# A logarithm series, a table load, two convolution inputs and two weight splits moved in the first layer of a Trainium2 encoder kernel

## The chip, the cores and the metric

One Trainium2 chip, one of its cores. The metric is the device time of one execution in microseconds (us). The kernel before takes 1221.76 us, the median of 3 runs (1221.18 to 1223.83).

The engines are named as the profile names them: PE is the matrix engine (PEld its weight loads), DVE the vector engine, ACT the scalar engine with its function tables, POOL the general engine, SP the queue that issues loads. Each works through its own instructions in order and waits for the others by semaphores. PSUM is the memory that PE writes to, here 8 banks of 128 x 512 float32; everything else lies in SBUF. "Wh" and "wl" below are the two halves into which a float32 weight is split so that PE can multiply it.

## The reference

Two layers on 512 positions of width 1024. Layer 0 mixes with a gated linear recurrence (RG-LRU), layer 1 with stick-breaking attention; each is followed by a SwiGLU block of width 2816, with an RMS norm ahead of every block and at the end. Only layer 0's mixer is touched by the change:

```python
h = rmsnorm(x, g)                       # rsqrt of the mean square, per position
gate_br, x_br = split(h @ w_in)         # 1024 + 1024 columns
xc = causal_conv(x_br, conv_w) + conv_b # 4 taps along the positions
r = sigmoid(blockdiag(xc, w_r) + b_r)   # 4 blocks of 256
i = sigmoid(blockdiag(xc, w_i) + b_i)
log_a = 8 * r * log_sigmoid(lam)        # lam: one number per channel
a = exp(log_a)
u = sqrt(max(-expm1(2 * log_a), 0)) * (i * xc)
hs = scan(a, u)                         # h_t = a_t h_{t-1} + u_t
x = x + (hs * gelu(gate_br)) @ w_out
```

## The kernel before, in words

Everything is kept transposed: 128 channels on the partitions, 512 positions along the row. A 128 x 1024 piece of weights is a *chunk*. SP loads it (raw), ACT copies it to a rounded half (wh, L136), and DVE or POOL subtracts that from the raw data (wl, L137). A product is then three matmuls for each 128 x 128 block: wh by the high half of the input (L165), wh by the low half (L166), wl by the high half (L167). Three buffers each for wh and wl and four for raw limit how far this runs ahead. Which engine makes wl is written down for the first 20 chunks in a table, `wl_on` (L58), and alternates afterwards.

Layer 0's mixer is the function `rglru`, and its chunks come in this order: m = 0 to 6 of the x branch (chunks 0 to 6), the gate weights of block 0 (7), m = 7 (8), gate weights of block 1 (9), then g = 0 and 1 of the gate branch (10, 11), gate weights of block 2 (12), g = 2 (13), gate weights of block 3 (14), g = 3 to 7 (15 to 19), and then the 8 chunks of the output product. PE takes them in that order, without a break if its inputs are there and its target bank is free. Banks are handed out in turn: x tiles 0 to 3 go to banks 70 to 73, the norm's sums to 74, x tile 4 to 75, the broadcast to 76, tiles 5 and 6 to 77 and 70; the gates of block 0 take 71 to 74, tile 7 takes 75 again, the gates of block 1 76, 77, 70, 71, g = 0 and 1 take 72 and 73, the gates of block 2 74 to 77, g = 2 takes 70, the gates of block 3 71 to 74. A bank can be written again only when its last reader is done.

The norm is not applied to the input. ACT squares the input tiles (L235), DVE adds the squares up (`acc`, L237), and in the middle of tile 3 PE sums `acc` over the partitions (`norm_rs1`, L255). ACT takes the square root of the sum (L242), DVE refines its reciprocal in five small operations (L243 to L247) and writes it on four diagonals (L249). In the middle of tile 4 PE multiplies the diagonals with ones (`norm_rs2`, L263), ACT copies the result (L264): `rsB`, the factor of each position, the same in all partitions. Every x tile is multiplied with it when it is taken out of PSUM.

That is `evac_x` (L324): DVE multiplies bank and rsB (L330), into a tile `xb` in SBUF for m < 4 and in place in PSUM for the others; ACT writes the first tap and the bias to xc (L331); DVE adds the three other taps to xc, one operation each (L333); ACT rounds xc (ah, L335), DVE subtracts (al, L336). For m < 4 the bank is free after the first of these, for the others after the third tap.

`decay` (L310) computes 8 log_sigmoid(lam) for 8 columns of 128 channels: a reciprocal, a square, and a series of ten terms in Horner's form, a multiplication and an addition for each term, all on 128 x 8 elements, each step on the result of the one before. Its result is first needed by the gates of block 0.

After the gates (sigmoids on ACT, L357 and L358, and a multiplication on POOL, L359), `chain` computes a and the square root on ACT and the scans on DVE (L373, L374), four tiles at a time. The gate branch's tiles are multiplied by rsB on DVE (`gt`, L432) and, for g < 5, kept in SBUF so that the bank is free.

The scheduler orders each engine's instructions by the program's order, priorities and `tc.issue_after`, which holds instructions back until a given one has been placed.

Of the kernel before, what the change touches and what calls it, by code (L numbers as in the profile page):

```python
# [13 lines left out]
AF = mybir.ActivationFunctionType  # L14
ALU = mybir.AluOpType
# [23 lines left out]
def ts(i, n=P):  # L39
    return slice(i * n, (i + 1) * n)  # L40


class Kern:
    def __init__(self, ctx, tc, a, out):
        self.ctx, self.tc, self.nc, self.a, self.out = ctx, tc, tc.nc, a, out
        mk = lambda name, bufs, **kw: ctx.enter_context(tc.tile_pool(name=name, bufs=bufs, **kw))
        self.const = mk("const", 1)
        self.wp = mk("wp", 1)
        self.tp = mk("tp", 1)
        self.ar = mk("ar", 1)  # L50
        self.free = deque(range(NSLOT))
        self.slot = {}
        pp = mk("pp", 1, space=bass.MemoryType.PSUM)
        self.bank = [pp.tile([P, S], F32, name=f"bank{i}") for i in range(8)]
        self.bi = 0
        self.tn = 0
        self.wl_dve = False
        self.wl_on = {**dict.fromkeys((*range(5, 12), 14, 15, 16), self.nc.gpsimd),  # L58
                      **dict.fromkeys((2, 3, 4, 12, 13, 17, 18, 19), self.nc.vector)}

    def ps(self):
        b = self.bank[self.bi % 8]
# [235 lines left out]
    def rglru(self):  # L298
        nc, tc = self.nc, self.tc
        with ExitStack() as cx:  # L300
# [4 lines left out]
            cl, w, z, z2, pl = (sm[:, ts(i, 8)] for i in range(5))  # L305
# [4 lines left out]
            def decay():  # L310
                nc.vector.tensor_scalar(z, w, 2.0, None, ALU.add)
                nc.vector.reciprocal(z, z)
                nc.vector.tensor_tensor(z, z, w, ALU.mult)
                nc.vector.tensor_tensor(z2, z, z, ALU.mult)
                nc.vector.tensor_scalar(pl, z2, 2.0 / 21, 2.0 / 19, ALU.mult, ALU.add)
                for n in (17, 15, 13, 11, 9, 7, 5, 3, 1):
                    nc.vector.tensor_tensor(pl, pl, z2, ALU.mult)
                    nc.vector.tensor_scalar(pl, pl, 2.0 / n, None, ALU.add)
                nc.vector.tensor_tensor(pl, pl, z, ALU.mult)
                nc.vector.scalar_tensor_tensor(cl, lam, 0.0, pl, ALU.min, ALU.subtract)  # L320
                nc.vector.tensor_scalar(cl, cl, RG_C, None, ALU.mult)
                nc.vector.tensor_scalar(ncl, cl, -1.0, 0.0, ALU.mult, ALU.max)

            def evac_x(m, ps):  # L324
                xc[m], ah[m], al[m] = self.new("xc"), self.new("ah", F32R), self.new("al", F32R)
                cw = lambda j: self.col("cw", j * 8 + m)
                src = ps
                if m < 4:
                    ps = self.new("xb")
                nc.vector.tensor_tensor(ps, src, self.rsB, ALU.mult)  # L330
                nc.scalar.activation(xc[m], ps, AF.Identity, scale=cw(3), bias=self.col("cb", m))  # L331
                for d in (1, 2, 3):
                    nc.vector.scalar_tensor_tensor(xc[m][:, d:], ps[:, :S - d], cw(3 - d), xc[m][:, d:],  # L333
                                                   ALU.mult, ALU.add)
                nc.scalar.copy(ah[m], xc[m])  # L335
                nc.vector.tensor_tensor(al[m], xc[m], ah[m].bitcast(F32), ALU.subtract)  # L336
                if m < 4:
                    self.rel(ps)

            def tile_x(m, mid=None):  # L340
                p = self.ps()
                self.mm_tile(p, self.u, mid)
                return p

            def gates(n, prev=None):
                wh, wl = self.chunk()
                for j in range(2):
                    m = 2 * n + j
                    pr, pi = self.ps(), self.ps()
                    for g, pt in ((0, pr), (1, pi)):  # L350
                        for k in range(2):
                            o = (g * 2 + j) * 2 + k
                            self.mm3(pt, wh[:, ts(o)], wl[:, ts(o)], ah[2 * n + k], al[2 * n + k], k == 0, k == 1)
                    r[m], sv[m] = self.new("r"), self.new("sv")
                    iv = self.tmp()
                    with tc.issue_after(prev.ins) if prev else ExitStack():
                        nc.scalar.activation(r[m], pr, AF.Sigmoid, bias=self.col("br", m))  # L357
                        nc.scalar.activation(iv, pi, AF.Sigmoid, bias=self.col("bi", m))  # L358
                    nc.gpsimd.tensor_tensor(xc[m], iv, xc[m], ALU.mult)  # L359
                    self.last = nc.scalar.activation(sv[m], r[m], AF.Tanh, scale=ncl[:, m:m + 1])  # L360
# [28 lines left out]
            def tile_x2():  # L389
                p = (self.ps(), self.ps())  # L390
                raws = [self.raw.pop(i)[0] for i in range(2)]
                hl = [self.split_tiles(i) for i in range(2)]
                for k in range(KT):
                    self.norm_in(k, "g_mix0", False)
                    for i in range(2):
                        if k % 2 == 0:
                            self.split_piece(i, raws[i], *hl[i], slice(k * P, (k + 2) * P))
                        self.mm3(p[i], hl[i][0][:, ts(k)], hl[i][1][:, ts(k)], *self.u[k], k == 0, k == KT - 1)
                for i in range(2):
                    self.wq.pop(i)  # L400
                self.used = 2
                return p

            pend = []
            for m in range(KT):
                if m == 0:
                    with tc.manual_schedule(engines={mybir.EngineType.Activation, mybir.EngineType.DVE}):
                        pend = list(enumerate(tile_x2()))
                    continue
                if m == 1:  # L410
                    continue
                pend.append((m, tile_x(m, {3: self.norm_rs1, 4: self.norm_rs2}.get(m))))
                if m == 2:
                    with tc.issue_after(self.uhi.ins):
                        for k in range(KT):
                            self.norm_sq(k, nc.vector)
                elif m == 3:
                    with tc.issue_after(self.dgi.ins):
                        decay()
                if m >= 4:  # L420
                    for q in pend[:3]:
                        evac_x(*q)
                    pend = pend[3:]
                if m in (6, 7):
                    gates(m - 6)
            for q in pend:
                evac_x(*q)
# [430 lines left out]
```

## Time and profile before

| what | us |
|---|---|
| median of 3 runs | 1221.76 |
| the profiled execution, as a run | 1221.93 |
| its span, first to last instruction | 1220.1 |
| PE busy in it | 1167.0 |
| DVE, ACT and POOL busy in it | 586.0, 521.4, 463.8 |

Between the run's time and the span lie 1.8 us. The times of instructions below count from the start of the span. A row of the timeline gives start, duration, engine, line, operation, output and inputs, and in square brackets the idle time of the engine before it and who ended it; "x3" is three like operations in a row, merged. A matmul's duration overlaps with the next one's, so what counts for PE is the distance from start to start.

### The profile page before, as it was taken

The page shows a single profiled execution, that of the slowest core. Times are in us where ns is not written, and L with a number is a line of the kernel's source. Part 1 is how long each engine was busy: PE and PEld are TensorE (multiplying, and loading weights), DVE is VectorE, ACT ScalarE, POOL GpSimd, SP SyncE. Part 2 cuts the span into 40 slices and gives each one's busy share as a digit, 9 for nine tenths or more (in the row PEclk, how much of TensorE's full clock was granted, in tenths as well). Part 3 has the DMA queues.
Part 4 walks back from the last instruction along what each step waited for, and adds up shares of the span by engine and source line. Part 5 has one row for each costly group of instructions (what it writes and reads, how often), then busy time and mean ns, then how long its engine had stood idle before and what let it go on. Part 6 is the DMA issues. An engine that isn't in the chain of part 4 may idle for free.

```text
span 1220.1 us, 13748 instructions
## 1 busy us (share of the span) xinstructions
PE 1167.0 (96%) x5347; PEld 956.8 (78%) x5347; DVE 586.0 (48%) x797; ACT 521.4 (43%) x750; POOL 463.8 (38%) x285
## 2 busy tenths in 40 slices
PE   9899999999999999999978888799999999999996
PEld 6687788888888888888866766578888888888886
DVE  6977743323323222222799999985332332321112
ACT  6497443323323222223677777654332332332221
POOL 2353343333333323321166666524333333332332
PEclk9999999999999999999999999999999999999998
DMA  7222322232322333332111011113223232233321
GB/s 243 70 84 84 100 97 93 97 99 91 104 96 93 93 97 95 98 103 91 52 48 36 35 35 53 35 53 103 94 96 100 90 104 96 93 93 97 95 63 69
DMA packets 31313, 105.80 MB, mean 87 GB/s; under 512 B 3600, under 2 KB 4624, under 8 KB 31248
## 3 DMA queue, kind: packets, MB, share of 16 engines
q1 hardware_dynamic: 30960, 104.40, 26.6%
q8 instruction: 42, 0.69, 0.2%
q10 hardware_dynamic: 288, 0.52, 0.1%
q14 instruction: 23, 0.19, 0.0%
HBM read 102.81 MB, written 2.10 MB: 86 GB/s over the span
## 4 chain that ended last, share of the span: by engine, by line
PE 74%; DVE 13%; issue 3%; ACT 2%; POOL 0%; DVEq 0%; ACTq 0%; POOLq 0%
PE bank L165 24%; PE bank L167 24%; PE bank L166 24%; DVE sph L637 2%; DVE t L636 2%; DVE wl L137 2%; DVE r L643 1%; DVE awh L679 1%; PE bank L663 1%; DVE ql L591 1%; DVE ks L598 1%; DVE t L577 1%; DVE o L702 1%; DVE awl L684 1%; DVE bank L382 0%
## 5 line engine op out<-in xcount | busy, mean ns | idle before, releaser
L136 ACT CAST wh<-raw 128x1024 fp32r<-128x1024 f32 (+2 forms) x202 | 203.3, 1009 | 534.5 <-PE bank L166 281.0
L165 PE MATMUL bank<-uh,wh 128*128 128x512 f32 x960 | 377.8, 394 | 13.7 <-DVE t L577 8.1
L167 PE MATMUL bank<-uh,wl 128*128 128x512 f32 x960 | 374.5, 390 | 1.0 <-DVE wl L137 1.0
L166 PE MATMUL bank<-ul,wh 128*128 128x512 f32 x960 | 374.7, 390 | 0.3 <-DVE ul L220 0.3
L137 POOL TENSOR_TENSOR wl<-raw,wh 128x1024 fp32r<-128x1024 f32 (+2 forms) x97 | 225.6, 2326 | 366.8 <-ACT wh L136 362.5
L165 PEld LDWEIGHTS bank<-uh,wh 128*128 128x128 f32 x960 | 181.0, 188 | 53.3 <-issue 15.2
L167 PEld LDWEIGHTS bank<-uh,wl 128*128 128x128 f32 x960 | 180.6, 188 | 39.3 <-DVE wl L137 1.4
L166 PEld LDWEIGHTS bank<-ul,wh 128*128 128x128 f32 x960 | 180.9, 188 | 37.8 <-DVE ul L220 0.9
L137 DVE TENSOR_TENSOR wl<-raw,wh 128x1024 fp32r<-128x1024 f32 (+2 forms) x105 | 132.6, 1266 | 139.4 <-ACT wh L136 138.4
L469 POOL TENSOR_TENSOR fl<-t,fh 128x512 fp32r<-128x512 f32 x44 | 67.3, 1529 | 198.1 <-ACT fh L468 198.1
L165 PE MATMUL bank<-fh,wh 128*128 128x512 f32 (+1 forms) x374 | 141.1, 377 | 0.0
L166 PE MATMUL bank<-fl,wh 128*128 128x512 f32 (+1 forms) x374 | 140.8, 376 | 0.0
L167 PE MATMUL bank<-fh,wl 128*128 128x512 f32 (+1 forms) x374 | 140.8, 376 | 0.0
L465 DVE TENSOR_TENSOR t<-bank,rsB 128x512 f32<-128x512 f32 x44 | 30.4, 691 | 199.4 <-PE bank L167 199.4
L463 DVE TENSOR_TENSOR t<-bank,rsB 128x512 f32<-128x512 f32 x44 | 30.4, 691 | 117.1 <-PE bank L167 117.1
L638 POOL TENSOR_TENSOR spl<-t,sph 128x512 fp32r<-128x512 f32 (+1 forms) x48 | 58.9, 1231 | 65.4 <-DVE sph L637 51.6
L165 PEld LDWEIGHTS bank<-fh,wh 128*128 128x128 f32 x374 | 70.4, 188 | 13.0
L166 PEld LDWEIGHTS bank<-fl,wh 128*128 128x128 f32 x374 | 70.4, 188 | 12.8
L167 PEld LDWEIGHTS bank<-fh,wl 128*128 128x128 f32 x374 | 70.4, 188 | 12.8
L237 POOL TENSOR_TENSOR acc<-acc,t 128x512 f32<-128x512 f32 x24 | 38.6, 1608 | 52.1 <-ACT t L235 43.4
L684 POOL TENSOR_TENSOR awl<-t,awh 128x512 fp32r<-128x512 f32 x28 | 40.0, 1427 | 41.2 <-DVE awh L679 41.2
L491 DVE TENSOR_TENSOR x<-x,bank 128x512 f32<-128x512 f32 x15 | 10.3, 687 | 74.7 <-PE bank L167 74.7
(165 smaller groups left out, 1464.3 us busy)
## 6 DMA issues: line engine op xcount, KB each, us to landing
raw<-w_gu SPq DMA_DIRECT2D x88, 512.0 KB, 3.5
raw<-w_dn SPq DMA_DIRECT2D x32, 448.0 KB, 3.3
raw<-w_dn SPq DMA_DIRECT2D x16, 512.0 KB, 3.5
raw<-w_qk SPq DMA_DIRECT2D x16, 512.0 KB, 3.4
raw<-w_in SPq DMA_DIRECT2D x14, 512.0 KB, 3.7
raw<-w_ao SPq DMA_DIRECT2D x8, 512.0 KB, 3.5
raw<-w_v SPq DMA_DIRECT2D x8, 512.0 KB, 3.4
raw<-w_bo SPq DMA_DIRECT2D x8, 512.0 KB, 3.4
```

Source lines behind the costliest of these rows:

```text
L136: self.nc.scalar.copy(wh[:, c], raw[:, c])
L137: self.wl_engine(i).tensor_tensor(wl[:, c], raw[:, c], wh[:, c].bitcast(F32), ALU.subtract)
L165: mm(out, lhsT=wh, rhs=xh, start=first, stop=False)
L166: mm(out, lhsT=wh, rhs=xl, start=False, stop=False)
L167: mm(out, lhsT=wl, rhs=xh, start=False, stop=last)
L237: self.acci = eng.tensor_tensor(self.acc, self.acc, sq, ALU.add)
L463: nc.vector.tensor_tensor(tg, pg, self.rsB, ALU.mult)
L465: nc.vector.tensor_tensor(tu, pu, self.rsB, ALU.mult)
L469: nc.gpsimd.tensor_tensor(al[f], tu, ah[f].bitcast(F32), ALU.subtract)
L636: nc.vector.scalar_tensor_tensor(sp[:, :w], z, 0.0, e[:, :w], ALU.max, ALU.add)
L638: nc.gpsimd.tensor_tensor(sl[:, :w], sp[:, :w], sh[:, :w].bitcast(F32), ALU.subtract)
L684: eng.tensor_tensor(wl[:, :w], ts_[i][:, :w], hd["wh"][i][:, :w].bitcast(F32), ALU.subtract)
```

## The change

Four edits.

- The series: each term is now one operation, (pl + 2/n) * z2, where it was a multiplication and an addition: 27 small operations become 18.
- The series is issued behind the last addition of `acc` (`acci`), no longer behind the last diagonal (`dgi`).
- ACT takes the root of one dummy element behind the squares, so that the table of the square root is loaded there and not in front of L242.
- The tiles m = 2 and 3 are multiplied by rsB in place in PSUM, as m = 4 to 7 were; `xb` is left for m = 0 and 1. The wl of chunks 15 and 16 (g = 3 and 4) goes from POOL to DVE.

```diff
-        self.wl_on = {**dict.fromkeys((*range(5, 12), 14, 15, 16), self.nc.gpsimd),
-                      **dict.fromkeys((2, 3, 4, 12, 13, 17, 18, 19), self.nc.vector)}
+        self.wl_on = {**dict.fromkeys((*range(5, 12), 14), self.nc.gpsimd),
+                      **dict.fromkeys((2, 3, 4, 12, 13, 15, 16, 17, 18, 19), self.nc.vector)}
...
-                nc.vector.tensor_scalar(pl, z2, 2.0 / 21, 2.0 / 19, ALU.mult, ALU.add)
-                for n in (17, 15, 13, 11, 9, 7, 5, 3, 1):
-                    nc.vector.tensor_tensor(pl, pl, z2, ALU.mult)
-                    nc.vector.tensor_scalar(pl, pl, 2.0 / n, None, ALU.add)
-                nc.vector.tensor_tensor(pl, pl, z, ALU.mult)
+                nc.vector.tensor_scalar(pl, z2, 2.0 / 21, None, ALU.mult)
+                for n in (19, 17, 15, 13, 11, 9, 7, 5, 3):
+                    nc.vector.scalar_tensor_tensor(pl, pl, 2.0 / n, z2, ALU.add, ALU.mult)
+                nc.vector.scalar_tensor_tensor(pl, pl, 2.0, z, ALU.add, ALU.mult)
...
-                if m < 4:
+                if m < 2:
                     ps = self.new("xb")
...
-                if m < 4:
+                if m < 2:
                     self.rel(ps)
...
                         for k in range(KT):
                             self.norm_sq(k, nc.vector)
-                elif m == 3:
-                    with tc.issue_after(self.dgi.ins):
+                        nc.scalar.activation(self.st[:, 0:1], self.ones[:, 0:1], AF.Sqrt)
+                    with tc.issue_after(self.acci.ins):
                         decay()
```

From here on lines of the changed kernel are one lower than before from L318 on: L329 there is L330 here, L332 is L333, L335 is L336, L431 is L432.

Where the series stands on DVE before, between the norm's sums and the first x tile (sm holds the series' values, st and rsT the norm's):

```order
L237 TENSOR_TENSOR acc<-acc,t_300 128x512
L243 TENSOR_SCALAR st<-bank_74 128x4
L244 RECIPROCAL st<-st 128x4
L245 SCALAR_TENSOR_TENSOR st<-st 128x4
L246 TENSOR_TENSOR st<-st 128x4
L247 SCALAR_TENSOR_TENSOR rsT<-st 128x4
L249 TENSOR_SCALAR t_325<-ident,rsT 128x128 x4
L311 TENSOR_SCALAR sm<-sm 128x8
L312 RECIPROCAL sm<-sm 128x8
```

The same place on DVE in the changed kernel, four small steps (L312 to L315) left out at the dots:

```order
L237 TENSOR_TENSOR acc<-acc,t_300 128x512
L311 TENSOR_SCALAR sm<-sm 128x8
...
L317 SCALAR_TENSOR_TENSOR sm<-sm 128x8 x7
L243 TENSOR_SCALAR st<-bank_74 128x4
L317 SCALAR_TENSOR_TENSOR sm<-sm 128x8
L244 RECIPROCAL st<-st 128x4
...
L247 SCALAR_TENSOR_TENSOR rsT<-st 128x4
L320 TENSOR_SCALAR sm<-sm 128x8
L249 TENSOR_SCALAR t_344<-ident,rsT 128x128
L321 TENSOR_SCALAR sm<-sm 128x8
L249 TENSOR_SCALAR t_344<-ident,rsT 128x128 x3
```

Twelve steps of the series now stand ahead of the norm's first small operation, and the other six between its operations; none stands behind the last diagonal.

The x tiles 2 to 4 on DVE in the changed kernel, from the third tile's second tap on (xc_42, xc_45 and xc_48 are tiles 2, 3 and 4; the bank's number is the last two digits):

```order
L332 SCALAR_TENSOR_TENSOR xc_42_424<-bank2_72,par_86,xc_42_424 128x510
L329 TENSOR_TENSOR bank3_73<-bank3_73,rsB_129 128x512
L332 SCALAR_TENSOR_TENSOR xc_42_424<-bank2_72,par_86,xc_42_424 128x509
L329 TENSOR_TENSOR bank5_75<-bank5_75,rsB_129 128x512
L332 SCALAR_TENSOR_TENSOR xc_45_464<-bank3_73,par_86,xc_45_464 128x511
L335 TENSOR_TENSOR al_44_426<-xc_42_424,ah_43_425 128x512
L332 SCALAR_TENSOR_TENSOR xc_45_464<-bank3_73,par_86,xc_45_464 128x510
L332 SCALAR_TENSOR_TENSOR xc_48_474<-bank5_75,par_86,xc_48_474 128x511
L332 SCALAR_TENSOR_TENSOR xc_45_464<-bank3_73,par_86,xc_45_464 128x509
L332 SCALAR_TENSOR_TENSOR xc_48_474<-bank5_75,par_86,xc_48_474 128x510
```

The order of the tiles is that of before; what moved is what they read: before, the rows of tiles 2 and 3 read xb, and bank 73 was free after its first row.

The scans of tiles 2 and 3 and what follows them on DVE, before:

```order
L374 SCALAR_TENSOR_TENSOR sv_72_666<-r_71_665,xc_46_473 128x512
L432 TENSOR_TENSOR gt_79_762<-bank3_73,rsB_129 128x512
L432 TENSOR_TENSOR gt_86_838<-bank0_70,rsB_129 128x512
L137 TENSOR_TENSOR wl17_945<-raw17_812,wh17_944 128x1024
L368 SCALAR_TENSOR_TENSOR sv_81_783<-t93_885,sv_81_783 128x512
```

and in the changed kernel:

```order
L373 SCALAR_TENSOR_TENSOR sv_70_656<-r_69_655,xc_45_464 128x512
L431 TENSOR_TENSOR gt_77_752<-bank3_73,rsB_129 128x512
L137 TENSOR_TENSOR wl15_831<-raw15_726,wh15_830 128x1024
L431 TENSOR_TENSOR gt_84_828<-bank0_70,rsB_129 128x512
L137 TENSOR_TENSOR wl16_903<-raw16_758,wh16_902 128x1024
L137 TENSOR_TENSOR wl17_935<-raw17_802,wh17_934 128x1024
```

The two wl stand behind the multiplication of g = 1, the one that frees bank 73, and are gone from POOL, where they stood ahead of the multiplications by the input gate of tiles 5 and 6.

## The prediction

> **What bounds the kernel now.** I read the page first, then the waits of PE over the first 160 us, which hold the mixer, then the timelines of PE, DVE, POOL and ACT around each wait.
>
> ```profile
> PE 1167.0 (96%) x5347; PEld 956.8 (78%) x5347; DVE 586.0 (48%) x797; ACT 521.4 (43%) x750; POOL 463.8 (38%) x285
> ...
> PE bank L165 <- DVE xc L333: 5.4, 1, 5.4
> PE bank L165 <- DVE gt L432: 1.5, 1, 1.5
> ...
> PE bank L166 <- DVE al L384: 1.1, 1, 1.1
> PE bank L167 <- DVE wl L137: 1.0, 1, 1.0
> ```
>
> PE is busy in 96% of the span, and behind the mixer nothing is edited: what PE loses by waiting in the mixer is lost at the end, and what it no longer loses is gained. In the mixer it waits four times for more than 1 us or about that: for a third tap of the convolution, for the multiplication of g = 1, and later for al and wl. The rows of PE at the first two:
>
> ```profile
> 32.89 1.06 PE L263 MATMUL bank<-t,ones 128*128 128x128 f32 x8
> ...
> 50.15 0.39 PE L165 MATMUL bank<-ah,wh 128*128 128x512 f32 x1
> ...
> 52.65 0.39 PE L167 MATMUL bank<-ah,wl 128*128 128x512 f32 x1
> 58.39 0.77 PE L165 MATMUL bank<-uh,wh 128*128 128x512 f32 x1 [5.36 <-DVE xc L333]
> ...
> 62.07 0.40 PE L165 MATMUL bank<-uh,wh 128*128 128x512 f32 x1
> ...
> 95.20 0.39 PE L167 MATMUL bank<-ah,wl 128*128 128x512 f32 x1
> 97.13 0.50 PE L165 MATMUL bank<-ah,wh 128*128 128x512 f32 x1 [1.54 <-DVE gt L432]
> ```
>
> From 50.15 to 52.65 there are 11 steps, 0.227 us each. The matmul at 62.07 is the tenth of tile 7; without a break it would have started at 52.65 + 10 x 0.227 = 54.92. So the first wait costs 7.15 us: 5.51 of waiting and 1.64 because PE comes back slow (nine steps in 3.68 us, 0.41 each). The second wait costs 97.13 - 95.43 = 1.70 and 0.11 more for a first matmul of 0.50 in place of 0.39: 1.81 us, with no slow stretch behind it.
>
> Why the third tap of tile 4 is late is in DVE's rows, beside those of POOL:
>
> ```profile
> 21.70 3.08 DVE L237 TENSOR_TENSOR acc<-acc,t 128x512 f32<-128x512 f32 x4
> 27.79 0.16 DVE L243 TENSOR_SCALAR st<-bank 128x4 f32<-128x4 f32 x1 [3.01 <-ACT st L242]
> 27.87 0.17 DVE L244 RECIPROCAL st<-st 128x4 f32<-128x4 f32 x1
> ...
> 31.11 0.17 DVE L318 TENSOR_SCALAR sm<-sm 128x8 f32<-128x8 f32 x1
> 31.32 2.36 DVE L317 TENSOR_TENSOR sm<-sm 128x8 f32<-128x8 f32 x1
> ...
> 36.04 0.68 DVE L330 TENSOR_TENSOR xb<-bank,rsB 128x512 f32<-128x512 f32 x1
> ...
> 39.45 2.38 DVE L322 TENSOR_SCALAR sm<-sm 128x8 f32<-128x8 f32 x1
> ...
> 50.33 0.69 DVE L330 TENSOR_TENSOR bank<-bank,rsB 128x512 f32<-128x512 f32 x1
> 50.93 0.74 DVE L333 SCALAR_TENSOR_TENSOR xc<-xb,par,xc 128x511 f32<-128x511 f32 x1
> 51.59 0.68 DVE L336 TENSOR_TENSOR al<-xc,ah 128x512 fp32r<-128x512 f32 x1
> 52.19 0.74 DVE L333 SCALAR_TENSOR_TENSOR xc<-xb,par,xc 128x510 f32<-128x510 f32 x1
> 52.85 0.74 DVE L333 SCALAR_TENSOR_TENSOR xc<-bank,par,xc 128x511 f32<-128x511 f32 x1
> 53.51 2.22 DVE L333 SCALAR_TENSOR_TENSOR xc<-xb,par,xc 128x509 f32<-128x509 f32 x1
> ...
> 57.51 0.74 DVE L333 SCALAR_TENSOR_TENSOR xc<-bank,par,xc 128x509 f32<-128x509 f32 x1
> ```
>
> ```profile
> 24.88 2.38 POOL L137 TENSOR_TENSOR wl<-raw,wh 128x1024 fp32r<-128x1024 f32 x1 [10.77 <-ACT wh L136]
> 31.27 2.39 POOL L137 TENSOR_TENSOR wl<-raw,wh 128x1024 fp32r<-128x1024 f32 x1 [4.01 <-ACT wh L136]
> ...
> 52.85 2.34 POOL L137 TENSOR_TENSOR wl<-raw,wh 128x1024 fp32r<-128x1024 f32 x1 [4.24 <-PE bank L166]
> ...
> 90.40 2.85 POOL L137 TENSOR_TENSOR wl<-raw,wh 128x1024 fp32r<-128x1024 f32 x1
> 93.21 2.21 POOL L359 TENSOR_TENSOR xc<-t,xc 128x512 f32<-128x512 f32 x1
> ```
>
> Three things are seen. DVE has no gap here from 36.04 on and starts its tiles only when the series lets it. A DVE operation that takes all its data from SBUF stands still while POOL works: 0.17 us become 2.36 beside POOL's 31.27, a *hold* of 2.2 us; the tap from xb at 53.51 takes 2.22 instead of 0.74. And the tap from a bank at 52.85, under the same POOL operation, takes 0.74: with a PSUM input there is no hold.
>
> **The change part by part.** Steps from start to start: L330 50.33 to 50.93, 0.60; a tap 0.66 (50.93 to 51.59); al 0.60 (51.59 to 52.19); a small step that needs the one before 0.205 (31.11 to 31.32), one that doesn't 0.08 (27.79 to 27.87).
>
> *The table.* ACT's rows, with the broadcast's copy and the first bias of tile 7, used below:
>
> ```profile
> 23.75 1.05 ACT L136 CAST wh<-raw 128x1024 fp32r<-128x1024 f32 x1 [1.85 <-PE bank L166]
> 24.82 1.28 ACT L242 ACT_TABLE_LOAD   x1
> ...
> 33.98 0.59 ACT L264 COPY rsB<-bank 128x512 f32<-128x512 f32 x1 [2.79 <-PE bank L263]
> ...
> 67.88 0.78 ACT L331 ACTIVATE xc<-bank,par 128x512 f32<-128x512 f32 x1 [1.30 <-DVE bank L330]
> ```
>
> Before, the load ran from 24.82 to 26.10 and the root waited on for PE's sums: hidden. Now 1.28 and a dummy of a few tenths lie in the 1.85 us in which ACT waits for PE anyway. Worth nothing either way; were the gap missing, the wh behind it would come up to 1.5 us later, for a chunk that PE needs only with tile 5, whose turn comes after 32.89, the middle of tile 4.
>
> *The series.* It starts at 24.7 behind the last addition, in DVE's gap of 3.01. Its second operation, at 24.9, meets POOL's 24.88 and is held to about 27.28. Ten dependent steps later, at 27.3 + 9 x 0.205 = 29.2, comes L243 (before: 27.79). The norm's and the series' operations now alternate and hide each other's delay, 0.205 a pair: five pairs bring the first diagonal to 30.25, the three others at 0.22 each end near 31.1. PE wants them at 32.89, so this costs nothing, with 1.8 us to spare, but only 0.15 us before POOL's 31.27. Behind the diagonals nothing is left of the series; rsB is there at 34.57, and the first L330 starts at 34.6 instead of 36.04. L322's hold at 39.45 is not saved: POOL's next wl then stops a tap from xb.
>
> *Two more tiles in PSUM.* Their six taps can no longer be held; the price is that banks 72 and 73 are free only after the third tap. By the order of the changed kernel, up to tile 3's third tap DVE does 5 multiplications, 13 taps and 3 al: 5 x 0.60 + 13 x 0.66 + 3 x 0.60 = 13.38, and one hold of 2.2 among the taps from xb: 15.6. From 34.6 that gives 50.18 for the next start, and the tap itself ends 0.08 later, 50.26. PE wants bank 73 for the gates of block 0 at 50.15: a wait of 0.15 with the semaphore, and 0.11 for the restart. Bank 72 is needed at 48.8 and free at 46.4. Tile 4's third tap follows after 2 x 0.66 + 2 x 0.60 = 2.52, ending at 52.8, where before it began at 57.51; PE wants bank 75 at 52.88, now 53.1. The wait of 5.36 is gone, and with it the slow stretch: 7.15 - 0.26 = 6.9 us gained.
>
> [...]
>
> *The two wl.* The second wait is for g = 1's multiplication, behind two multiplications and two scans that POOL holds:
>
> ```profile
> 83.03 2.33 DVE L374 TENSOR_TENSOR_SCAN sv<-r,xc 128x512 f32<-128x512 f32 x2
> ...
> 86.39 4.59 DVE L373 TENSOR_TENSOR xc<-xc,sv 128x512 f32<-128x512 f32 x2
> 90.91 5.59 DVE L374 TENSOR_TENSOR_SCAN sv<-r,xc 128x512 f32<-128x512 f32 x2
> 96.42 1.25 DVE L432 TENSOR_TENSOR gt<-bank,rsB 128x512 f32<-128x512 f32 x2
> ```
>
> Two scans without POOL take 2.33. Without the wl of 90.40 POOL goes straight to the multiplication now at 93.21 (1.2 us by itself), from 91.0 to 92.2, and the scans end at 94.4: g = 1's multiplication starts at 94.4 instead of 96.42 and ends at 95.1, against PE's wish at 95.43. These are times of before; ACT, DVE and POOL all move forward with tile 7, PE with its own gain. PE gains 6.9; the chain starts with ACT's bias of tile 7, at 67.88 before. I carry the queue on from 52.8: taps and al of tiles 4 to 6 to 58.15, two al that alternate with two POOL multiplications to 60.6, L329 to 61.3: 6.6 earlier. So 0.3 of PE's lead is not matched, the slack of 0.3 covers it, and I leave 0.15 for a restart: 1.81 - 0.15 = 1.65 gained. The wl themselves add 2 x 1.2 us to DVE behind that point, before the wl of chunk 17, for which DVE waits idle already; PE needs chunk 15 only after block 3's gates. The waits for wl and al later in the mixer hang on chains that start with PE's block 3 gates: they move with PE and stay.
>
> Sum: 6.9 + 1.65 = 8.5 us. The profiled execution, 1221.93, stands 0.17 above the median; from the median, 1221.76 - 8.5 = **1213.2**.
>
> **The rivals.** *The diagonals miss the gap* (0.14). If the series takes 0.2 us longer than I add up, POOL's 31.27 catches one to four diagonals until 33.5; PE then waits at 32.89, 0.9 to 1.6 us, and rsB and everything behind it shift with PE, so that it is paid once: up to 1214.8. The 0.15 us of margin speak for it. [...]
>
> *The second wait stays* (0.11). If the chain of tile 7 gains less than PE, g = 1 is late as before: 1221.76 - 6.9 = 1214.9.
>
> *The wait moves to bank 73* (0.10). If DVE is held twice more before tile 3's third tap, that is 4.4 us, PE waits 4.5 for bank 73, and, as that is near the wait after which it was slow, loses another 1.6: 1219.3, which is no gain that can be told; with one hold, about 1215.5. The sum above has no reserve: 50.26 against 50.15.
>
> *Slower* (0.03). The series ahead of the diagonals makes the broadcast the bound: from a delay of about 11 us at 32.89 on, more than the 8.5 gained and 2.4. That would need about 1.1 us for each of the 12 small steps ahead of L243; they take 0.205, and two holds together make 4.4.
>
> *More* (0.04). The wait for wl at about 118, 1.0 and a restart, goes too: 8.96 + 1.1 gives 1211.7.
>
> **How the numbers follow.** The forecast, 1212.5 to 1214.2 as the two remainders are 0 or 1 us, has 0.58. The range takes in the better case, the first two rivals and the milder half of the third: 1211.6 to 1216.8. A measurement of this kernel tells about 0.2%, 2.4 us, from no change: faster needs less than 1219.3. The third rival at its worst and a failure of the series' move give 0.05 for the same, 0.03 for slower, 0.92 for faster.
>
> **What would show it.** In the new profile: no wait of PE for a tap above 0.5 us, no steps of 0.41 behind it; the first L329 at 34.6; the diagonals done before 31.27; tile 3's third tap ending near 50.3; no row of `gt` among PE's waits. A PE wait at L263, or DVE rows of 2.2 us and more among the taps from a bank, would prove me wrong.

## The result and the profile after

| | before | after |
|---|---|---|
| median, us (4 runs each) | 1221.47 | 1214.55 |
| lowest to highest | 1220.34 to 1223.83 | 1211.87 to 1214.85 |
| the profiled execution, its span | 1221.93, 1220.1 | 1214.85, 1213.1 |
| mixer stretch in it | 108.25 | 100.56 |

The changed kernel is faster by 0.6%: ratio of the runs 0.9936, 95% interval 0.9916 to 0.9956 (the two medians alone give 0.9943). Forecast were 1213.2 us, 0.9930 of the 1221.76 known then, and a range of 1211.6 to 1216.8. "Mixer stretch" is used for all kernels below: from PE's first matmul behind the norm's sums (L255) to the last matmul of the mixer that PE had to wait for (before: from 27.32 to 135.57). From there to the first matmul of the SwiGLU block it is 38.7 us in both. The stretch is the better measure of a small edit, since the start of L255 itself lies anywhere from 25.88 to 29.19 us in the profiles of this study, and at 27.32 and 27.92 in two profiles of one and the same kernel. It goes in part with the landing of the second of x's eight tiles: ACT, which waits for that load, starts on the tile at 6.84 us before and at 7.13 after. After is 0.65 us later there than before (27.16 and 26.51): 7.69 - 0.65 = 7.04 is the 7.08 between the profiled executions.

PE's waits from the norm's sums to the middle of the output product, in the changed kernel (engine, line, who ended the wait and at which line; us in total, times, longest):

```profile
PE bank L166 <- DVE al L383: 1.1, 1, 1.1
PE bank L167 <- DVE wl L137: 1.0, 1, 1.0
PE bank L165 <- DVE gt L431: 0.4, 1, 0.4
PE bank L165 <- ACT ah L382: 0.2, 1, 0.2
```

The tap's 5.4 us are gone, the 1.5 for `gt` have become 0.4, the rest is as it was. PE's rows at those places:

```profile
27.16 0.95 PE L255 MATMUL bank<-ones,acc 128*128 128x1 f32 x8
27.97 0.48 PE L165 MATMUL bank<-uh,wh 128*128 128x512 f32 x1
...
50.58 0.39 PE L167 MATMUL bank<-ah,wl 128*128 128x512 f32 x1
50.99 0.47 PE L165 MATMUL bank<-ah,wh 128*128 128x512 f32 x1
51.30 0.39 PE L166 MATMUL bank<-al,wh 128*128 128x512 f32 x1
...
81.26 0.39 PE L166 MATMUL bank<-ul,wh 128*128 128x512 f32 x1
81.65 0.50 PE L167 MATMUL bank<-uh,wl 128*128 128x512 f32 x1
81.98 0.39 PE L165 MATMUL bank<-uh,wh 128*128 128x512 f32 x1
...
89.26 0.39 PE L167 MATMUL bank<-ah,wl 128*128 128x512 f32 x1
90.08 0.50 PE L165 MATMUL bank<-ah,wh 128*128 128x512 f32 x1 [0.43 <-DVE gt L431]
90.42 0.39 PE L166 MATMUL bank<-al,wh 128*128 128x512 f32 x1
...
128.53 0.51 PE L165 MATMUL bank<-ah,wh 128*128 128x512 f32 x1 [0.16 <-ACT ah L382]
```

Against a step of 0.227 PE loses 0.18 + 0.08 = 0.26 at bank 73 (50.99), 0.27 at the wl of chunk 13 (81.65), and 0.59 + 0.11 = 0.70 at g = 1 (90.08). A wait need not have brackets: the first two show only in the distance from start to start.

DVE at the norm and at the taps:

```profile
25.61 2.33 DVE L314 TENSOR_TENSOR sm<-sm 128x8 f32<-128x8 f32 x1
...
29.47 0.15 DVE L243 TENSOR_SCALAR st<-bank 128x4 f32<-128x4 f32 x1
...
30.74 0.68 DVE L249 TENSOR_SCALAR t<-ident,rsT 128x128 f32<-128x128 f32 x3
35.26 1.29 DVE L329 TENSOR_TENSOR xb<-bank,rsB 128x512 f32<-128x512 f32 x2 [3.84 <-ACT rsB L264]
...
37.06 6.19 DVE L332 SCALAR_TENSOR_TENSOR xc<-xb,par,xc 128x511 f32<-128x511 f32 x6
...
58.93 3.41 DVE L335 TENSOR_TENSOR al<-xc,ah 128x512 fp32r<-128x512 f32 x2
62.26 0.69 DVE L329 TENSOR_TENSOR bank<-bank,rsB 128x512 f32<-128x512 f32 x1
63.80 2.32 DVE L332 SCALAR_TENSOR_TENSOR xc<-bank,par,xc 128x511 f32<-128x511 f32 x3 [0.85 <-ACT xc L330]
```

The series is held once (25.61), the diagonals are done at 31.42, and the six taps from xb take 6.19 us with one hold in them; from then to 58.9 nothing on DVE is held. The two al at 58.93 are.

### The profile page after: what moved, and what is told of

Its sections match the earlier page's. It is cut to its first block, busy times and chain, and to the rows that moved or that the text cites. A ratio compares the mean times of both kernels' runs of the same rounds, so it can differ in the third digit from the quotient of the medians.

```text
span 1213.1 us, 13743 instructions
## 1 busy us (share of the span) xinstructions
PE 1165.5 (96%) x5347; PEld 955.4 (79%) x5347; DVE 581.4 (48%) x790; ACT 521.6 (43%) x751; POOL 457.8 (38%) x283
## 4 chain that ended last, share of the span: by engine, by line
PE 74%; DVE 14%; issue 3%; ACT 1%; POOL 0%; DVEq 0%; ACTq 0%; POOLq 0%
PE bank L165 24%; PE bank L167 24%; PE bank L166 24%; DVE sph L636 2%; DVE t L635 2%; DVE wl L137 2%; DVE r L642 1%; DVE awh L678 1%; DVE awl L683 1%; DVE o L701 1%; DVE ql L590 1%; DVE ks L597 1%; DVE t L576 1%; PE bank L662 1%; DVE t L641 0%
## 5 line engine op out<-in xcount | busy, mean ns | idle before, releaser
L137 POOL TENSOR_TENSOR wl<-raw,wh 128x1024 fp32r<-128x1024 f32 (+2 forms) x95 | 219.6, 2312 | 361.5 <-ACT wh L136 361.5
L137 DVE TENSOR_TENSOR wl<-raw,wh 128x1024 fp32r<-128x1024 f32 (+2 forms) x107 | 136.1, 1274 | 137.2 <-ACT wh L136 136.2
```

The source lines that it names most:

```text
L137: self.wl_engine(i).tensor_tensor(wl[:, c], raw[:, c], wh[:, c].bitcast(F32), ALU.subtract)
```

## The experiments

The theory: the gain is the two waits, each removed by its own edit (the taps in PSUM with the series out of the way; the two wl). The rivals: the head start of the series alone does it (H), or PSUM alone (P). All kernels are read by the mixer stretch; ratios are to the kernel before on the same chip.

| kernel | time | ratio, interval | stretch |
|---|---|---|---|
| before | 1221.47 | | 108.25 |
| after | 1214.55 | 0.9936, 0.9916 to 0.9956 | 100.56 |
| series alone | 1221.49 | 0.9995, 0.9985 to 1.0004 | 108.06 |
| PSUM alone | 1218.83 | 0.9975, 0.9966 to 0.9985 | 104.72 |
| PSUM alone, once more | 1218.55 (one run) | | 104.75 |
| the two wl alone | 1221.05 | 0.9993, 0.9984 to 1.0002 | 106.62 |
| after without the wl | 1217.72 | 0.9966, 0.9953 to 0.9979 | 104.16 |
| after without series and table | 1215.85 | 0.9944, 0.9927 to 0.9960 | 102.21 |
| after without the table | 1214.79 (one run) | | 101.12 |
| after with the long series | 1214.13 | 0.9931, 0.9916 to 0.9945 | 100.59 |
| after, multiplications on DVE | 1215.09 | 0.9936, 0.9921 to 0.9951 | 100.68 |
| all eight tiles in PSUM | 1213.06 | 0.9919, 0.9904 to 0.9934 | 99.25 |
| the same, once more | 1213.32 | 0.9922, 0.9908 to 0.9935 | 99.23 |
| the same, wl of chunk 18 on POOL | 1216.10 | 0.9955, 0.9942 to 0.9967 | 102.09 |

**One part at a time.** The series fused and issued behind `acci`, nothing else:

```diff
...
-                elif m == 3:
-                    with tc.issue_after(self.dgi.ins):
+                    with tc.issue_after(self.acci.ins):
                         decay()
```

> The series alone: one operation per term and behind the norm's sums; tiles 2 and 3 keep xb, the table and the wl stay as before. Theory (late third tap: head start and holds together): the first multiplication by rsB starts 1.4 us earlier, but the taps of tiles 2 and 3 read xb and are held by one or two of POOL's wl, 2.2 us each, so PE still waits 2 to 4.5 us for tile 4's third tap, perhaps slow behind it: gain 1 to 5 us. Rival H (the head start alone is the gain): 6.9 us, no wait for a tap. Rival P (the PSUM tiles alone are the gain): none.

DVE's rows at the norm in this kernel:

```profile
30.04 0.15 DVE L243 TENSOR_SCALAR st<-bank 128x4 f32<-128x4 f32 x1
...
30.70 2.34 DVE L247 SCALAR_TENSOR_TENSOR rsT<-st 128x4 f32<-128x4 f32 x1
33.08 0.87 DVE L249 TENSOR_SCALAR t<-ident,rsT 128x128 f32<-128x128 f32 x4
```

It gains 0.19 us, nothing that a measurement can tell. All 18 steps of the series stand ahead of L243 here, not alternating with the norm, so L247 starts just behind POOL's wl of 30.64 and is held, and PE waits 1.0 us at L263: the prediction's rival of the diagonals that miss the gap, here in fact. The wait for the tap falls from 5.36 to 3.54, with slow steps of 0.43 us behind it still, and the one for `gt` grows to 1.86; the sum is nil. The theory's wait of 2 to 4.5 us came, its gain of 1 to 5 did not, and rival H is out.

Tiles 2 and 3 in PSUM, nothing else:

```diff
-                if m < 4:
+                if m < 2:
```

> Tiles 2 and 3 in PSUM alone; the series, the table and the wl as before. Theory: DVE starts its tiles at 36.04 as before, the third tap of tile 3 ends near 52 (36.04 + 13.4 + 0.35 of small steps + one hold of 2.2), so PE waits near 1.9 us for bank 73 and no longer for tile 4's tap, with no slow stretch: gain about 5 us. Rival H: no gain. Rival P: 6.9 us.

PE's row at bank 73:

```profile
53.20 0.68 PE L165 MATMUL bank<-ah,wh 128*128 128x512 f32 x1 [1.91 <-DVE xc L333]
```

3.53 us gained, where about 5 was expected. PE waits 1.91 us for bank 73, as forecast. What was not expected are eight steps of 0.43 us behind that wait, about 1.6 us in all (below).

The two wl on DVE, nothing else:

```diff
-        self.wl_on = {**dict.fromkeys((*range(5, 12), 14, 15, 16), self.nc.gpsimd),
+        self.wl_on = {**dict.fromkeys((*range(5, 12), 14), self.nc.gpsimd),
...
```

> The wl of chunks 15 and 16 on DVE alone. Theory: PE and the chain of tile 7 stand to each other as before, the scans are held once less, and the wait for g = 1 (1.8 us with its restart) goes: gain 1.6 to 1.8 us, the wait of 5.4 us untouched. Rival (the wait for g = 1 hangs on ACT, not on POOL's wl): no gain.

PE's wait for the tap in this kernel:

```profile
59.15 0.77 PE L165 MATMUL bank<-uh,wh 128*128 128x512 f32 x1 [5.35 <-DVE xc L333]
```

The wait for `gt` is gone, the stretch is 1.63 shorter, and the wait for the tap is as it was. In the time it can't be told: the ratio's interval holds both 1 and the 0.9987 that 1.63 us make.

**One part left out.** The changed kernel with the wl of 15 and 16 back on POOL:

```diff
-        self.wl_on = {**dict.fromkeys((*range(5, 12), 14), self.nc.gpsimd),
+        self.wl_on = {**dict.fromkeys((*range(5, 12), 14, 15, 16), self.nc.gpsimd),
...
```

> The changed kernel with the wl of chunks 15 and 16 back on POOL. Theory: g = 1's multiplication comes 2 us later, PE waits 2.4 us for it instead of 0.43: gain over the kernel before 5 us where the whole change has 7. Rival (the wl are worth nothing): 7 us.

PE at the multiplication of g = 1:

```profile
91.76 0.50 PE L165 MATMUL bank<-ah,wh 128*128 128x512 f32 x1 [2.58 <-DVE gt L431]
```

The wait is near the 2.4 us that the theory gave, but slow steps of 0.43 us follow it, so that the edit is worth 3.60 here, not 2, where it was worth 1.63 alone. The single parts add up to 0.19 + 3.53 + 1.63 = 5.35 us, all together to 7.69.

The changed kernel without its series and table edits (long form, behind `dgi`):

```diff
...
-                        nc.scalar.activation(self.st[:, 0:1], self.ones[:, 0:1], AF.Sqrt)
-                    with tc.issue_after(self.acci.ins):
+                elif m == 3:
+                    with tc.issue_after(self.dgi.ins):
```

> The change without its two edits on the norm: the series in its old form at its old place, no early table load, but tiles 2 and 3 in PSUM and the two wl on DVE. Theory (the parts are worth more together, as each wait that stays also costs a slow stretch behind it): the wait at bank 73 of 1.9 us with its slow stretch of 1.6 stays, the wait for g = 1 goes: mixer stretch 102.7 to 103.3, so that the series with its place is worth about 2.4 us beside the other two edits, where alone it was worth 0.2. Rival (the series is worth nothing, as it was alone): 100.6 within 0.4.

102.21: the theory's direction, but below its 102.7 to 103.3; the wait of 1.91 us at bank 73 came without slow steps (0.23 us a step behind it). The series, worth nothing alone, and the table, which was not run alone, are worth 1.65 us here, nearly all of it that wait (2.30 - 0.41 between starts at bank 73, less the 0.27 that only the changed kernel loses at chunk 13). Rival P, that PSUM does it alone, falls with it.

The changed kernel with the long form of the series, 27 operations, at its new place:

```diff
...
-                for n in (19, 17, 15, 13, 11, 9, 7, 5, 3):
-                    nc.vector.scalar_tensor_tensor(pl, pl, 2.0 / n, z2, ALU.add, ALU.mult)
...
+                for n in (17, 15, 13, 11, 9, 7, 5, 3, 1):
+                    nc.vector.tensor_tensor(pl, pl, z2, ALU.mult)
+                    nc.vector.tensor_scalar(pl, pl, 2.0 / n, None, ALU.add)
...
```

> The changed kernel with the series in its old form (27 small operations, a multiplication and an addition for each term), still placed behind the last addition of acc. Theory (the form buys the few tenths by which the diagonals escape POOL's wl, and the head start of the first multiplication by rsB): as many steps as before stand ahead of L243, so the diagonals still end close to 31.9, but seven steps are left behind them and one is held, so the first multiplication of a tile starts about 0.4 us later and bank 73 is late by 0.3 to 0.7 us: mixer stretch 0.4 to 1.5 us above the changed kernel's 100.6. Rival (the form is worth nothing, only the place counts): 100.6 within 0.3.

DVE's rows from the last diagonals to the first x tile:

```profile
30.59 0.28 DVE L249 TENSOR_SCALAR t<-ident,rsT 128x128 f32<-128x128 f32 x1
...
31.18 2.24 DVE L318 TENSOR_SCALAR sm<-sm 128x8 f32<-128x8 f32 x1
...
34.06 0.17 DVE L322 TENSOR_SCALAR sm<-sm 128x8 f32<-128x8 f32 x1
34.32 1.29 DVE L330 TENSOR_TENSOR xb<-bank,rsB 128x512 f32<-128x512 f32 x2
```

The theory fails and its rival holds: 100.59. The diagonals end at 30.87, also ahead of POOL; the tail of the series is held as expected, but its last step ends at 34.23, when rsB is only just there (ACT's copy runs from 33.70 to 34.29). The nine operations saved, 9 x 0.205 = 1.85 us, were all in time that DVE had. In this kernel only the place counts. The long form without the dummy root was not run; there the whole series may stand ahead of L243 (next experiment), and its length could count.

The changed kernel without the dummy root:

```diff
-                        nc.scalar.activation(self.st[:, 0:1], self.ones[:, 0:1], AF.Sqrt)
```

> The changed kernel without the dummy root: the table of the square root is loaded in front of L242 again. Theory (the load lies in ACT's wait for the norm's sums either way): the 1.28 us of the load stand between the cast of a wh and L242, L242 still waits at least 1 us for PE, mixer stretch 100.6 within 0.3. Rival (the early load is part of the gain, because PE's second norm product follows ACT's root): L242 1.3 us later, PE waits at L263, mixer stretch 101.0 to 101.9.

DVE's rows at the norm, then ACT's, in that kernel:

```profile
27.52 1.77 DVE L317 SCALAR_TENSOR_TENSOR sm<-sm 128x8 f32<-128x8 f32 x9
...
30.02 0.15 DVE L243 TENSOR_SCALAR st<-bank 128x4 f32<-128x4 f32 x1
...
30.88 3.05 DVE L249 TENSOR_SCALAR t<-ident,rsT 128x128 f32<-128x128 f32 x4
```

```profile
24.82 1.28 ACT L242 ACT_TABLE_LOAD   x1
27.49 0.26 ACT L242 ACTIVATE st<-bank,eps 128x4 f32<-128x4 f32 x1 [1.39 <-PE bank L255]
```

On ACT the theory holds: the load is hidden, L242 waits 1.39 us for PE behind it, and its rival's late root did not come. But the stretch is 0.56 longer. The row of nine L317 says why: without the dummy the scheduler puts the whole series ahead of L243, as in the series alone; with it, in the changed kernel and in the one with the long series, the two alternate. In both kernels POOL's first wl holds the same step of the series, the fourth, so the order is what differs. The third diagonal then starts at 31.28, beside POOL's wl of 31.27, and is held, and PE stops in the middle of L263:

```profile
32.89 0.61 PE L263 MATMUL bank<-t,ones 128*128 128x128 f32 x4
33.79 0.71 PE L263 MATMUL bank<-t,ones 128*128 128x128 f32 x4 [0.29 <-DVE t L249]
```

From L255 to the matmul behind L263 it is 7.76 us, and 7.20 in the changed kernel: the 0.56. So the table edit works by the order that it brings about on another engine. That the scheduler expects the root later when a load stands in front of it is a likely reason, which no run here shows.

**Why the second wait stays by 0.70.** In the changed kernel POOL's two multiplications start at 58.79, 0.14 us ahead of the first of two al, and hold both (58.93, 3.41 us above). Moved to DVE:

```diff
-                    nc.gpsimd.tensor_tensor(xc[m], iv, xc[m], ALU.mult)
+                    (nc.gpsimd if n else nc.vector).tensor_tensor(xc[m], iv, xc[m], ALU.mult)
```

> The changed kernel with the two multiplications by the input gate of block 0 on DVE, no longer on POOL (1.2 us each). Theory (the multiplication of g = 1 is late by 0.70 because POOL's two multiplications, starting 0.1 us ahead of the first al, hold DVE's two al and so put off tile 7 by about 1 us): the al take 0.7 each, tile 7 starts about 1 us earlier even with the two multiplications on DVE, the wait for g = 1 and the 0.27 at chunk 13 go: mixer stretch about 99.6 to 99.9. Rival (DVE has no room): the two multiplications cost on DVE what the hold cost, and the stretch stays at 100.6 within 0.3.

Tile 7 on DVE in this kernel, and what POOL does beside it:

```profile
60.20 0.69 DVE L329 TENSOR_TENSOR bank<-bank,rsB 128x512 f32<-128x512 f32 x1
60.80 2.29 DVE L335 TENSOR_TENSOR al<-xc,ah 128x512 fp32r<-128x512 f32 x1
63.02 1.52 DVE L332 SCALAR_TENSOR_TENSOR xc<-bank,par,xc 128x511 f32<-128x511 f32 x2
```

```profile
59.88 2.67 POOL L137 TENSOR_TENSOR wl<-raw,wh 128x1024 fp32r<-128x1024 f32 x1 [2.00 <-ACT wh L136]
```

The theory fails. Counted from L255 (26.19 here, 27.16 after), tile 7's multiplication starts at 34.01 in place of 35.10, 1.1 earlier, but its first tap at 36.83 in place of 36.64: POOL has come to its wl earlier, and that holds the al between them. One hold was swapped for another, and PE's wait for `gt` is 0.43 again. The rival's stretch came, 100.68, but not for its reason: it had DVE without room, and tile 7's multiplication did start earlier.

What removes it is one hold less before: all eight tiles in PSUM.

```diff
-                if m < 2:
-                    ps = self.new("xb")
...
-                if m < 2:
-                    self.rel(ps)
```

> The changed kernel with all eight x tiles multiplied by rsB in place in PSUM, no xb at all. Theory (what is left of the taps' lateness is one hold of 2.2 us on taps from xb, under the wl of chunk 7): the hold goes, the taps of tile 3 end about 2 us earlier, bank 73 is no longer late (0.27 us), tile 7's chain starts earlier, and the multiplication of g = 1, which was late by 0.70, is in time: mixer stretch about 99.3 in place of 100.6, time about 1.2 us under the changed kernel's. Rival (banks): bank 70 is then free only after tile 0's third tap, and PE waits for it at tile 6 or for 71 at the gates of block 0: no gain, or a loss of some tenths.

DVE's first rows behind the broadcast:

```profile
35.42 1.90 DVE L327 TENSOR_TENSOR bank<-bank,rsB 128x512 f32<-128x512 f32 x3 [3.84 <-ACT rsB L264]
37.22 4.68 DVE L330 SCALAR_TENSOR_TENSOR xc<-bank,par,xc 128x511 f32<-128x511 f32 x7
```

Seven taps take 4.68 us, where six from xb took 6.19. PE's waits are then these, and the losses of 0.26, 0.27 and 0.70 are all gone:

```profile
PE bank L166 <- DVE al L379: 1.1, 1, 1.1
PE bank L167 <- DVE wl L137: 1.0, 1, 1.0
PE bank L165 <- ACT ah L378: 0.2, 1, 0.2
```

The gain of 1.31 us in the stretch is the sum of these three, 1.23, within 0.1. Once more:

> All eight tiles in PSUM, no xb, once more, with more rounds. Theory (no tap can be held): mixer stretch 99.25 within 0.2 and a ratio to the kernel before of 0.9915 to 0.9930, against 0.9936 for the changed kernel. Rival (the gain of 1.3 us in the first profile is scatter): a ratio of 0.9930 to 0.9945.

Stretch 99.23, ratio 0.9922. That is the fastest version here, and beats the kernel before beyond doubt; against the changed kernel it is ahead by 1.3 us in both profiles' stretches, while the intervals of the ratios overlap.

The next wait on that version, for the wl of chunk 18:

```diff
-        self.wl_on = {**dict.fromkeys((*range(5, 12), 14), self.nc.gpsimd),
-                      **dict.fromkeys((2, 3, 4, 12, 13, 15, 16, 17, 18, 19), self.nc.vector)}
+        self.wl_on = {**dict.fromkeys((*range(5, 12), 14, 18), self.nc.gpsimd),
+                      **dict.fromkeys((2, 3, 4, 12, 13, 15, 16, 17, 19), self.nc.vector)}
```

> All eight tiles in PSUM, and in addition the wl of chunk 18 (g = 6), for which PE waits 1.2 us behind DVE's last scans, on POOL, which is idle there from 101 to 116 us. Theory (that wait is DVE's queue, not the data): wl is ready about 2 us earlier, the wait goes, though POOL holds one or two of DVE's scans for about 2 us; the mixer stretch falls by 0.5 to 1.5 us below 99.25. Rival (the hold gives it back): DVE's scans end 2 us later, gt and the first al of the output product with them, PE waits there instead, and the stretch is 99.0 or more, up to 100.5.

The multiplications ahead of DVE's last scans, the moved wl on POOL beside them, and PE in the output product:

```profile
106.84 3.42 DVE L368 TENSOR_TENSOR xc<-xc,sv 128x512 f32<-128x512 f32 x2
```

```profile
105.94 3.18 POOL L137 TENSOR_TENSOR wl<-raw,wh 128x1024 fp32r<-128x1024 f32 x1 [3.48 <-ACT wh L136]
```

```profile
129.88 0.50 PE L165 MATMUL bank<-ah,wh 128*128 128x512 f32 x1 [2.12 <-ACT ah L378]
```

The wait for the wl of chunk 18 is gone. But it is the rival, and worse than its bound: a hold of 2.2 us on DVE's multiplications (3.42 us, where the two at 103.38 take 1.29), a changed order of PE in the output product, and a wait of 2.12 us there with slow steps of 0.43 us behind it. (As the order differs, its stretch is taken from the SwiGLU's first matmul, 38.67 us back.) It is 2.8 us longer than without this edit, and so are the medians, 1216.10 against 1213.32.

The wait at bank 73 with PSUM alone, a second profile:

> The kernel with tiles 2 and 3 in PSUM alone, once more, for the slow stretch behind its wait at bank 73. Theory A (after a wait of 1.9 us it is open whether PE comes back slow, since one profile of this wait had the slow stretch and one, with the same instructions up to there, had none): the same wait of 1.9 us, with eight or so steps of 0.43 us behind it or without; without them the mixer stretch is 103.1, with them 104.7. Theory B (the length of the wait decides, and the other profile differed by something else): the slow steps are there again, 104.7 within 0.3. Only the case without them tells the two apart.

The slow steps are there again; what that leaves open is told at the end.

## Why the prediction was right, and where its terms were off

**The first wait: right in size.** 6.9 us were forecast, 7.15 - 0.26 = 6.89 came. Its steps hold once 0.65 us is taken off for the later start: the first L329 at 35.26 - 0.65 = 34.61 (forecast 34.6); one hold among the taps from xb; PE's matmul at bank 73 at 50.99 - 0.65 = 50.34, forecast 50.15 + 0.15. No slow stretch follows.

**The second wait: right in kind, mis-sized.** 1.65 were forecast, 1.81 - 0.70 - 0.27 = 0.84 came. The step that failed is "L329 to 61.3: 6.6 earlier". ACT's first tap of tile 7, the row that it was to move:

```profile
62.98 0.78 ACT L330 ACTIVATE xc<-bank,par 128x512 f32<-128x512 f32 x1 [1.70 <-DVE bank L329]
```

That is 62.33 without the later start, against 67.88: 5.55 earlier, not 6.6, while PE came 6.9 earlier. "Two al that alternate with two POOL multiplications" was put at 2.45 us; they took 3.33, and they began 0.13 us later. The multiplications on DVE then showed that this order is not all of it: with the al relieved of the two multiplications, POOL's next operation, the wl of 59.88, held DVE in that kernel (2.29 us for an al, where the one at 51.59 before takes 0.68), and tile 7's taps started no earlier. The slack of 0.3 was too thin for that, and of the signs named one failed: a row of `gt` stands among PE's waits. The other term held. From that tap to the multiplication of g = 1 the chain is 28.54 - 26.38 = 2.16 us shorter (96.42 - 67.88 before, 89.36 - 62.98 after), where 96.42 - 94.4 = 2.0 was forecast. So the condition of the rival "the second wait stays" came true, a chain that gains less than PE, and about half of its price was paid: 0.81 of 1.65 us.

**The sum.** 6.89 + 0.84 = 7.73 against 7.69 in the stretch; 8.5 was forecast. From the median before, 1221.47, that would be 1213.8; the measured median is 1214.55, lowest 1211.87, so the rest is within the scatter of the runs.

**The table: right on ACT, wrong in what it is worth.** "Worth nothing either way" looked only at ACT's time, where the load is hidden with and without. It is worth 0.56 us because it changes DVE's order at the norm. The prediction had put the alternating order down to the place of the series.

**The series: the place, not the form.** The rival of the diagonals had a margin of 0.15 us; it came to 0.50 (31.42 against POOL's 31.92), and of the two kernels where it did happen one paid the forecast price of 0.9 to 1.6, 1.25 with L247 held (34.33 - 25.88 = 8.45 us from L255 to the matmul behind L263, against 7.20); with one diagonal held it was 0.56. That the margin was wider than forecast is in part luck: the first hold caught the fourth step of the series here (25.61), where the forecast had the second. In the kernel with the multiplications on DVE it caught the first, at 24.76; there the last diagonal begins only 0.01 us ahead of POOL's wl of 30.95, and just escapes (the last three, from 30.55 on, take 0.68 us). The form has no part in the gain as long as the two orders alternate: the long one gives the same stretch.

**PSUM as a source.** The forecast counted a tap alike from either memory; the rows of before have 0.74 us for the one from xb at 52.19 and 0.74 for the one from the bank at 52.85. The rows of after agree: grouped by line, the 15 taps from a bank between 30 and 60 us take 738 ns each, and in the kernel with all taps in PSUM the first seven take 4.68 us, 0.66 from start to start, the step that the forecast took from the kernel before.

```profile
L332 DVE SCALAR_TENSOR_TENSOR xc<-bank,par,xc 128x511 f32<-128x511 f32 (+2 forms) x15 | 10.6, 738 | 0.3 <-ACT xc L330 0.3
```

**Parts that add up to less than the whole.** 5.35 us alone, 7.69 together. The wait that a single edit left brought slow steps with it, 1.6 us in the series alone and in PSUM alone, and an earlier PE meets a chain that has not come along: without the wl the wait for `gt` grows from 1.54 to 2.58 us. The series alone also lacked the table edit, and lost the 1.25 us at L263. PSUM left out of the changed kernel was not run, and neither was the table alone.

## What to carry to other kernels

Where one engine stands still while another works, count the holds between a fixed start and the wait that ends last, and take away one that lies early; moving an operation from the engine that holds to the one held paid here where it left one hold less (the two wl, 1.63 us alone), and gave nothing where the next operation held in its place (the multiplications, a stretch of 100.68 against 100.56). An edit on one engine can act through the order that a scheduler gives another one, so compare the order of every engine, edit by edit, before calling a part free. Judge an edit of a microsecond by a stretch of the trace between two fixed instructions, and leave parts out of the whole as well as trying them alone.

## What the runs showed of the hardware

After waits of the same length, 1.91 us, PE came back slow in two profiles and at full speed in one. PE from the end of the wait at bank 73 on, in the second profile of PSUM alone, and then in the changed kernel without series and table; the columns are the stretch, its length, PE's busy time and matmuls, the granted clock, and the DMA's share and rate:

```profile
52.80:56.60 3.80, 3.71 (x9) 0.55 0.39 133
56.60:60.00 3.40, 3.40 (x16) 1.00 0.05 13
```

```profile
51.90:55.40 3.50, 3.45 (x15) 1.00 0.40 139
55.40:59.00 3.60, 3.60 (x18) 1.00 0.05 17
```

Every engine has the same instructions in the same order in both kernels up to there, and both waits are 1.91 us; yet in one the granted clock is 0.55 over the first 3.80 us, with steps of 0.43 us from 53.20 to 56.60, in the other it is 1.00. The first profile of PSUM alone had the slow stretch as well (0.51 from 53.20 to 56.60). In the series alone it began only 1.2 us after PE had come back, behind five full-speed steps (58.43 against 57.20); it followed waits of 2.12, 2.58, 3.54 and 5.36 us, and none of 1.44, 1.54 and 1.86. What decides in a given execution stays open: no run here shows it. For a forecast it means that the same wait of 1.91 us cost 2.2 us at the full clock and 3.7 with the slow steps (the tenth matmul from its end on starts 4.46 and 6.01 us after the last one ahead of it, where ten steps of 0.227 make 2.27).
